# A shared ring of weight slots that is no longer cut short near the end of a layer

## The chip, the cores and the metric

The kernel runs on one core of a Trainium2 chip. The metric is device time in microseconds (us) of one execution, as the median of several timed runs. The profile is of one further execution; "span" is the time from its first to its last instruction.

## The reference, cut to what matters

A two-layer trunk. In each layer a mixer (gated linear attention, a Fourier mix and windowed attention, merged through gates) is followed by a hierarchical mixture of 16 experts. Layer 0 works on 512 rows (256 of x, 256 of the context), layer 1 on 256.

```python
def hierarchical_moe(h, w_router_group, w_router_expert, w1, w3, w2):
    ...
    out = jnp.zeros(h.shape, h.dtype)
    for e in range(MOE_EXPERTS):          # 16
        hid = jax.nn.silu(h @ w1[e]) * (h @ w3[e])
        out = out + (hid @ w2[e]) * gates[:, e:e + 1]
    return out

def trunk_layer(x, xc, ...):
    ...
    x = x + gate1[:, None, :] * y
    h2 = modulate(rms_norm(x, g_ffn), shift2, scale2)
    x = x + gate2[:, None, :] * hierarchical_moe(h2...)
```

Each token has two experts, so most products of the loop are zero. `w1[e]` and `w3[e]` are 1024 x 512, `w2[e]` is 512 x 1024, all in float32.

## The kernel before

The experts run as 16 places, in an order by their number of tokens. A place is big (B, up to 128 tokens, products of split high and low halves) or small (s, up to 64 tokens, plain float32 products of two weight halves side by side): `PLACES`, line 30, "BBBBsBBsBBsBBsss" in layer 0 and "BBBsssBssssBssss" in layer 1. The last three places are small in both layers.

**The weights** of one place come as six pieces of 1 MB, two each of w1, w3 and w2, 96 pieces a layer. `pieces_of` (line 1266) yields them in the order of use: of place q the second pieces of w1 and w3, then the first pieces of place q+1, then the two of w2 of place q. `wload` (239, its DMA has line 245) issues each load on SP's queue, which is worked off in order; a load whose slot is still being read holds all that stand behind it. Numbered #1 to #96, the last are: #85 and #86 w2 of place 13, #87 and #88 second w1 and w3 of place 14, #89 and #90 first w1 and w3 of place 15, #91 and #92 w2 of place 14, #93 and #94 second w1 and w3 of place 15, #95 and #96 w2 of place 15.

**The ring.** `ring` (1256) gives each piece the next slot in turn, 8 KB a partition. Layer 0 has 12 slots, in this order from #1: six of `ra`, two of `raw`, two of `rb0`, two of `rb1`. Layer 1 has 13: the free half of `x` first, six of `ra`, two of `raw`, one each of `rc`, `rb0`, `rb1`, `rc`. The four slots of `rb0`, `rb1` and `rc` are the spare ones (`self.spare`, 1383), marked True. `ring` counts pieces; once the count is over `CUT` = 84, spare slots that come to the head are dropped, so that layer 0 goes on with 8 slots and layer 1 with 9. The four spare slots then serve, in order, the outputs of places 14 and 15 (`last_y`, 1666) and the first two row blocks that are read back (`rows`, 1755).

**A small place** on TensorE: `pair` (line 1643) with w1 and w3, a first half for the next place in `begin` (1646) and a second half in the loop (1676). Then ACT copies and takes tanh (1693, 1655), DVE multiplies twice (1656, 1657), TensorE transposes (1662), DVE copies (1697), and TensorE takes w2 (`pair` again, written to tile `c`). Outputs of places 0 to 13 are scattered to the DRAM tensor `yb` by GpSimd's queue (1561). Those of 14 and 15 stay in memory as two halves each (ACT 1731, DVE 1732) and are put onto their rows by products with a one-hot tile `oh` (1774). The rows of `yb` are read back on SP's queue (1758), their two halves added on GpSimd (1759), added on TensorE by a product with the identity (1777), and the sum goes through gate and addition into x (1795, 1797). A branch (1783) to a general path for overfull experts stands before that; it isn't taken in the profile.

**Order and memory.** The kernel is written in a tile framework that orders each engine's instructions ahead of the run, by place in the source and by its own reckoning of when an instruction's inputs are there, and adds the semaphores. Pools are stacked on a left and a right side; a new tile waits until the tiles that lay on its bytes have been read. `ra` is on the left, after `moed`; `rb0` and `rb1` are on the right. Layer 1 opens `hhi`, `hlo`, `early`, then `ong` and `ssum` on the left where `moed` and `ra` of layer 0 lay. Its first steps are the norm of x (416, 407, 408, 525), transposes (537), scale and shift (546), the split into `hhi` (GpSimd, 550) and `hlo` (DVE, 551), and the first products (228).

Of the kernel before, what the change touches and what calls it, by code (L numbers as in the profile page):

```python
# [8 lines left out]
F32 = mybir.dt.float32  # L9
F32R = mybir.dt.float32r  # L10
# [9 lines left out]
P = 128  # L20
# [10 lines left out]
RING = (6, 7)  # L31
ONCE = (0, 2)
AHEADG = 2
CUT = 84
EXTRA = 2
EA = 8
EB = 1
# [77 lines left out]
def ts(i, n):  # L115
    return slice(i * n, (i + 1) * n)
# [12 lines left out]
class Net:  # L129
# [461 lines left out]
    def mixer(self, l, filler):  # L591
# [20 lines left out]
        if l:  # L612

            h = [hp.tile([P, 2, KD, SEQ], F32R, name=n) for n in ("hhi", "hlo")]
# [16 lines left out]
        s1 = ExitStack()  # L631
        yc = self.swa(s1)
        self.dump(f"y2{l}", yc[0].bitcast(F32))
        self.rings, self.ahead, self.slots, self.piece, self.gen = [], [], [], 0, self.pieces_of(l)
        if l:

            self.rings = [(Slot(self.x[:, 2:4].rearrange("p t d -> p (t d)")), False)]
            self.ahead = [next(self.gen) for _ in self.rings]
            n = EXTRA
            self.raws += [self.raw] + [self.pool(sh, "raw2", bufs=n)] * n  # L640
# [590 lines left out]
    def moe_pre(self, l, T, ww):  # L1231

        nt, ns = T // P, T // SEQ
        self.sh = ExitStack()
        self.dp = self.pool(self.sd, "moed")
        self.pos = self.dp.tile([P, 5, NE], F32, name="pos")
        self.nc.sync.dma_start(self.pos, self.io["k_pos"][:, l])
        self.h2b = self.dr.tile([T, D], F32, name=f"h2b{l}")
        n = RING[l] - len(self.slots + self.rings)
        new = [(t, False) for t in self.slots] + [(self.pool(self.sd, "ra", bufs=n), False)] * n  # L1240
        self.rings = new + [(self.raw, False)] * 2 + self.rings
        self.once = [self.pool(self.sd, "rc", bufs=ONCE[l])] * ONCE[l] if ONCE[l] else []
        if self.once:
            ww.append(self.wload(self.io["w_out"][l][:, ts(3, 256)], KD, 256, self.once[0].tile([P, 2048], F32, name="wraw")))
        self.sx = ExitStack()
        self.xp = xp = self.pool(self.sx, "moex")
        self.h2 = xp.tile([P, nt, D], F32, name="h2")
        self.oh0 = xp.tile([P, nt, CAP[l]], F32, name="oh0")
        self.hp = hp = self.pool(self.sh, "moeh", side="right")
        self.xtr = [hp.tile([P, 2, 2, P], F32, name=f"xtr{i}") for i in range(3)]  # L1250
        self.g2 = self.mod_bcast(hp, l, 2, ns, "gm2")
        self.s2 = self.mod_bcast(hp, l, 1, ns, "sh2")
        self.ssq = hp.tile([P, ns, 2, 4], F32, name="ssq")
        self.pieces = chain(self.ahead + [next(self.gen) for _ in new], self.gen)

    def ring(self):

        self.piece += 1
        if self.piece > CUT:

            while self.rings[0][1]:
                self.rings.pop(0)
        self.rings.append(self.rings.pop(0))
        return self.rings[-1][0].tile([P, 2048], F32, name="wraw")

    def pieces_of(self, l):

# [108 lines left out]
    def moe_ahead(self, l):  # L1376


        n = 2 - l
        y1 = self.pool(self.sd, "rb1", bufs=n, side="right")  # L1380
        y0 = self.pool(self.sd, "rb0", bufs=n, side="right")

        self.spare = self.once[1:] + [y0] * n + [y1] * n + self.once[:1]
        self.rings[2:2] = [(p, True) for p in self.spare]
        gen = self.pieces

        first = [next(gen) for _ in range(len(self.rings) - ROWS[l].count("w"))]
        last = self.wd
        for o in ROWS[l]:
            if o == "w":  # L1390
                with self.tc.issue_after(last.ins):
                    first.append(next(gen))
                last = self.wd
            else:
                self.behind(self.hw[int(o)], last)
                last = self.hw[int(o)]
        self.pieces = chain(first, gen)
        self.got, self.cut, self.parts = {}, {}, 6
        self.cut["w1", 0, 0] = list(self.halves("w1", 0, 0))

    def moe(self, l):
# [263 lines left out]

        def last_y(e):

            ye = self.spare.pop(0).tile([P, 2048], F32, name="wraw").bitcast(F32R).rearrange("p (h d) -> p h d", h=2)
            yes.append(ye)
            return ye  # L1670
        p1 = begin(0, xx)
        for e in range(NE):
# [34 lines left out]
            if e == NE - 2:  # L1707
# [9 lines left out]
                rq = self.pool(sr, "rows2", bufs=2, side="right") if nt > 2 else None  # L1717
            if not big[e]:
                p2 = self.c2()
                for c in range(2):  # L1720
                    w = self.piece_at("w2", e, c)
                    for k in range(2):
                        pair(p2, hs, [w[:, k:k + 1, ts(o, 512)] for o in range(2)], (2 * c + k, 4), 1)
                if e < NE - 2:
                    ye = yp.tile([P, 512], F32, name="ye")
                    nc.scalar.activation(ye, p2, AF.Copy, scale=gsl[:, e:e + 1])  # L1726
                    put = (ye, e)
                    continue

                ye = last_y(e)[:, :, :512]  # L1730
                nc.scalar.activation(ye[:, 0], p2, AF.Copy, scale=gsl[:, e:e + 1])
                V.scalar_tensor_tensor(ye[:, 1], p2, gsl[:, e:e + 1], ye[:, 0].bitcast(F32), op0=OP.mult, op1=OP.subtract)
                continue
# [7 lines left out]
            if e < NE - 2:  # L1741
                ye = yp.tile([P, D], F32, name="ye")
                for o in range(2):
                    nc.scalar.activation(ye[:, ts(o, 512)], p2[o], AF.Copy, scale=gsl[:, e:e + 1])
                put = (ye, e)
                continue
            ye = last_y(e)
            for o in range(2):
                q = ts(o, 512)
# [4 lines left out]

        def rows(t):

            yr = (self.spare.pop(0) if t < 2 else rq).tile([P, 2048], F32, name="wraw").rearrange("p (r d) -> p r d", r=2)
            nc.sync.dma_start(yr, yb.rearrange("(r q) d -> q r d", r=2)[ts(t, P)])
            i = nc.gpsimd.tensor_add(yr[:, 0], yr[:, 0], yr[:, 1])
            self.adds += [i] if t >= 2 else []  # L1760
            return yr
        self.adds, self.lates = [], []
        yrs = [rows(t) for t in range(nt)]

        def put_rows(t, pt, js):
# [16 lines left out]
        n = nc.values_load(cnti[0:1, 0:1], min_val=0, max_val=T)  # L1782
# [3 lines left out]
        for t in range(nt):  # L1786
            self.pri.append(tc.cur_priority)
            yr = yrs[t]
# [125 lines left out]
```

## Time and profile before

| | |
|---|---|
| median of three timed runs | 1590.89 us (1585.81 to 1591.39) |
| profiled execution | 1584.03 us, its span 1582.0 us |
| PE, matmuls | 1452.4 us busy, 92% |
| DVE, ACT, POOL | 942.1, 752.1, 232.5 us busy |
| DMA | 363.14 MB, mean 230 GB/s |
| weight pieces of the experts | 192 loads of 1024 KB on SP's queue |
| experts of layer 0, experts of layer 1 | end near 940 us, near 1563 us |

The page gives the busy time of each engine, then the span in 40 slices of 39.55 us. A busy TensorE is not yet one at its peak, and the DMA digit is a mean over 16 DMA engines. SP is not counted as busy: its waits are read from its own view of the waits. A line such as L1643 or L245 belongs to a helper that many steps share, so a stretch of time has to go with it.

### The profile page before, as it was taken

The numbers are of one execution on the slowest core, as the hardware profiler recorded it, in microseconds if no ns is written. First come the engines' busy times: TensorE is split into PE (matmuls) and PEld (weight loads), VectorE is DVE, ScalarE is ACT, GpSimd is POOL, SyncE is SP. The second block draws the span as 40 slices with busy tenths as digits, with TensorE's granted clock in tenths as the row PEclk, the third lists the DMA queues.
The fourth block names the chain that finished last, engine by engine and source line by source line (L and its number), as shares of the span: only waits on it lengthen the run. The fifth ranks groups of instructions, "written<-read, shape, count | busy, mean of one in ns | idle before, by whom it ended". The sixth has DMA issues, their size and how long they took to land. (4 is left out here: it accounts for less than half of the span.)

```text
span 1582.0 us, 22237 instructions
## 1 busy us (share of the span) xinstructions
PE 1452.4 (92%) x8141; PEld 1020.5 (65%) x8141; DVE 942.1 (60%) x1753; ACT 752.1 (48%) x1292; POOL 232.5 (15%) x244
## 2 busy tenths in 40 slices
PE   6999899999999997899998979999899979998885
PEld 4666666577777796676675427687689967453421
DVE  4479667532376786797775417467965679251412
ACT  4668556422223233586665306668654548241411
POOL 2025100000021103111110014023001121121001
PEclk9999999999999997999999988999999989999998
DMA  9762242443556578699999763322336689999992
GB/s 321 214 208 92 91 150 81 145 138 110 198 174 214 187 234 311 214 357 388 391 369 369 289 256 116 122 90 81 105 100 200 214 309 337 370 384 393 395 373 89
DMA packets 218505, 363.14 MB, mean 230 GB/s; under 512 B 25676, under 2 KB 100630, under 8 KB 218388
## 3 DMA queue, kind: packets, MB, share of 16 engines
q1 hardware_dynamic: 211520, 349.77, 63.6%
q0 software_dynamic: 6432, 11.76, 2.1%
q8 instruction: 67, 1.10, 0.3%
q14 instruction: 50, 0.41, 0.1%
q10 hardware_dynamic: 436, 0.10, 0.0%
HBM read 350.56 MB, written 21.82 MB: 235 GB/s over the span
## 5 line engine op out<-in xcount | busy, mean ns | idle before, releaser
L266 DVE TENSOR_TENSOR wlo<-wraw,whi 128x1024 fp32r<-128x1024 f32 (+1 forms) x324 | 377.2, 1177 | 186.3 <-ACT whi L265 121.5
L265 ACT ACTIVATE whi<-wraw 128x1024 fp32r<-128x1024 f32 (+1 forms) x324 | 321.7, 1009 | 239.4 <-PE pa L229 114.6
L228 PE MATMUL pa<-hhi,whi 128*128 128x512 f32 (+1 forms) x704 | 240.6, 356 | 1.8 <-ACT qT L788 1.0
L229 PE MATMUL pa<-hlo,whi 128*128 128x512 f32 (+1 forms) x704 | 237.6, 352 | 0.0
L228 PEld LDWEIGHTS pa<-hhi,whi 128*128 128x128 f32 x704 | 133.3, 189 | 36.5 <-issue 16.0
L1643 PE MATMUL pa<-wraw,xh 128*64 128x512 f32 x520 | 151.4, 636 | 0.0
L231 PE MATMUL pa<-hhi,wlo 128*128 128x512 f32 (+1 forms) x704 | 151.0, 348 | 0.0
L229 PEld LDWEIGHTS pa<-hlo,whi 128*128 128x128 f32 x704 | 133.4, 190 | 22.6 <-issue 9.6
L231 PEld LDWEIGHTS pa<-hhi,wlo 128*128 128x128 f32 x704 | 113.4, 190 | 20.2 <-issue 6.2
L763 POOL TENSOR_TENSOR m<-m,gu 128x512 f32<-128x512 f32 (+1 forms) x32 | 39.3, 1228 | 402.7 <-DVE gu L761 402.7
L1656 DVE SCALAR_TENSOR_TENSOR th<-th,pa 64x512 f32<-64x512 f32 (+1 forms) x32 | 21.7, 679 | 124.2 <-ACT th L1655 124.2
L1643 PEld LDWEIGHTS pa<-wraw,xh 128*64 128x64 f32 x520 | 42.8, 144 | 76.5 <-issue 74.5
L235 PE MATMUL pa<-whi,xh 128*128 128x512 f32 x208 | 85.0, 408 | 7.4 <-ACT whi L265 6.9
L236 PE MATMUL pa<-wlo,xh 128*128 128x512 f32 x208 | 85.8, 413 | 2.9 <-DVE wlo L266 2.8
L237 PE MATMUL pa<-whi,xl 128*128 128x512 f32 x208 | 83.4, 401 | 0.0
L1555 POOL DMA_INDIRECT xg<-h2b,tki x30 | 35.7, 1190 | 264.5 <-PE c L1618 94.6
L1643 PE MATMUL c<-wraw,hh 128*64 128x512 f32 x256 | 72.6, 634 | 1.0 <-DVE hh L1697 1.0
L236 PE MATMUL pa<-y,whi 128*128 128x512 f32 (+1 forms) x192 | 66.3, 345 | 0.9 <-DVE y L272 0.9
L235 PE MATMUL pa<-y,whi 128*128 128x512 f32 (+1 forms) x192 | 65.5, 341 | 0.7 <-DVE mx L1143 0.7
L237 PE MATMUL pa<-y,wlo 128*128 128x512 f32 (+1 forms) x192 | 65.1, 339 | 0.0
L349 DVE SCALAR_TENSOR_TENSOR adaw<-adaw,cT 128x512 f32<-128x512 f32 x56 | 49.1, 877 | 15.8 <-DMA adaw<-in_w_ada_dram 15.2
L1561 POOL DMA_INDIRECT yb<-ye,yki x28 | 28.5, 1018 | 198.5 <-ACT ye L1726 109.1
(458 smaller groups left out, 2817.5 us busy)
## 6 DMA issues: line engine op xcount, KB each, us to landing
wraw<-in_w_dram SPq DMA_DIRECT2D x184, 1024.0 KB
wraw<-in_w_in_dram SPq DMA_DIRECT2D x44, 1024.0 KB
adaw<-in_w_ada_dram SPq DMA_DIRECT2D x80, 512.0 KB
adaw<-in_w_ada_dram SPq DMA_DIRECT2D x8, 1024.0 KB
wraw<-in_w_out_dram SPq DMA_DIRECT2D x8, 1024.0 KB
x<-in_w_dram SPq DMA_DIRECT2D x8, 1024.0 KB
yb<-zero SPq DMA_DIRECT2D x12, 512.0 KB
wraw<-yb SPq DMA_DIRECT2D x6, 1024.0 KB
```

Source lines behind the costliest of these rows:

```text
L228: mm(out, lh, rh, start=(i == 0), stop=False)
L229: mm(out, lh, rl, start=False, stop=False)
L231: self.mm = mm(out, ll, rh, start=False, stop=(i == len(ops) - 1))
L235: mm(out, lh, rh, start=start, stop=False)
L236: mm(out, lh, rl, start=False, stop=False)
L237: self.mm = mm(out, ll, rh, start=False, stop=stop)
L265: self.sp = nc.scalar.activation(hv[:, :, q], v[:, :, q], AF.Copy)
L266: self.sl = self.lo.tensor_sub(lv[:, :, q], v[:, :, q], hv[:, :, q].bitcast(F32))
L349: nc.vector.scalar_tensor_tensor(v[:, j], v[:, j], ck, acc, op0=OP.mult, op1=OP.add)
L763: nc.gpsimd.tensor_add(self.m[:, j, :], self.m[:, j, :], u[:, :TY])
L1555: return nc.gpsimd.indirect_dma_start(out=xgs[e % len(xgs)][:n], out_offset=None, in_=h2b, in_offset=bass.IndirectOffsetOnAxis(ap=tki[:n, ...
L1643: nc.tensor.matmul(ps[ts(i, SM)], xs[:, k0[0] + k, :], w[:, k, :], start=(k0[0] + k == 0), stop=(k0[0] + k == k0[1] - 1))
```

## The change

The mark on ring entries, the count and the cut go. All slots stay in the ring to the end of the layer, and what took spare slots by name now takes the ring's next slot at its place in the source: the output of place 14 between #92 and #93, that of place 15 and row blocks 0 and 1 after #96. In layer 0 the slots are then: output of place 14 that of #81 (as before), #93 to #95 those of #82 to #84, #96 that of #85, output of place 15 that of #86, row blocks those of #87 and #88. In layer 1: #88 to #91 those of #75 to #78, #92 that of #79, output of place 14 that of #80, #93 to #96 those of #81 to #84, output of place 15 that of #85, row blocks those of #86 and #87 (`raw`).

```diff
-CUT = 84
@@ mixer
-        self.rings, self.ahead, self.slots, self.piece, self.gen = [], [], [], 0, self.pieces_of(l)
+        self.rings, self.ahead, self.slots, self.gen = [], [], [], self.pieces_of(l)
         if l:
-            self.rings = [(Slot(self.x[:, 2:4].rearrange("p t d -> p (t d)")), False)]
+            self.rings = [Slot(self.x[:, 2:4].rearrange("p t d -> p (t d)"))]
@@ moe_pre
-        new = [(t, False) for t in self.slots] + [(self.pool(self.sd, "ra", bufs=n), False)] * n
-        self.rings = new + [(self.raw, False)] * 2 + self.rings
+        new = self.slots + [self.pool(self.sd, "ra", bufs=n)] * n
+        self.rings = new + [self.raw] * 2 + self.rings
@@ ring
-        self.piece += 1
-        if self.piece > CUT:
-
-            while self.rings[0][1]:
-                self.rings.pop(0)
         self.rings.append(self.rings.pop(0))
-        return self.rings[-1][0].tile([P, 2048], F32, name="wraw")
+        return self.rings[-1].tile([P, 2048], F32, name="wraw")
@@ moe_ahead
-        self.spare = self.once[1:] + [y0] * n + [y1] * n + self.once[:1]
-        self.rings[2:2] = [(p, True) for p in self.spare]
+        self.rings[2:2] = self.once[1:] + [y0] * n + [y1] * n + self.once[:1]
@@ last_y
-            ye = self.spare.pop(0).tile([P, 2048], F32, name="wraw").bitcast(F32R).rearrange("p (h d) -> p h d", h=2)
+            ye = self.ring().bitcast(F32R).rearrange("p (h d) -> p h d", h=2)
@@ rows
-            yr = (self.spare.pop(0) if t < 2 else rq).tile([P, 2048], F32, name="wraw").rearrange("p (r d) -> p r d", r=2)
+            yr = (self.ring() if t < 2 else rq.tile([P, 2048], F32, name="wraw")).rearrange("p (r d) -> p r d", r=2)
```

## Rows read from the trace of the kernel before

**Rows 1.** The page, part 2: DMA busy tenths in 40 slices.
```profile
DMA  9762242443556578699999763322336689999992
```

**Rows 2.** Waits of SP's queue, 885 to 935: who, for whom, total us, times, longest.
```profile
SPq L245 <- PE c L1643: 16.2, 2, 15.1
...
SPq L1758 <- DMA yb<-ye,yki: 3.8, 1, 3.8
```

**Rows 3.** The same view, 1495 to 1550.
```profile
SPq L245 <- PE c L1643: 13.3, 4, 10.5
```

**Rows 4.** Windows: length; busy us (instructions) by engine; granted clock, DMA share, GB/s.
```profile
902.90:908.00 5.10, 5.10 (x26) 1.66 (x24) 0.00 (x0) 0.00 (x0) 0.00 (x0) 0.94 0.07 12
908.00:920.70 12.70, 9.84 (x36) 3.08 (x32) 1.78 (x3) 1.87 (x3) 0.99 (x1) 0.73 1.01 373
...
1513.00:1517.70 4.70, 4.70 (x25) 1.57 (x23) 0.00 (x0) 0.69 (x1) 0.99 (x1) 1.00 0.74 268
1517.70:1544.50 26.80, 21.07 (x88) 6.87 (x86) 3.58 (x6) 3.54 (x6) 0.98 (x1) 0.87 1.03 393
```

**Rows 5.** Timeline of SP: start us, us, instruction, out<-in, count; three narrow windows.
```profile
906.33 0.37 SPq L245 DMA_DIRECT2D wraw<-in_w_dram  x1
...
910.64 1.22 SPq L245 DMA_DIRECT2D wraw<-in_w_dram  x2
...
915.71 1.99 SPq L1758 DMA_DIRECT2D wraw<-yb  x4
```

**Rows 6.** Timeline of PE, layer 0; in brackets idle time before and what ended it.
```profile
892.39 4.50 PE L1643 MATMUL pa<-wraw,xh 128*64 128x512 f32 x18
...
907.43 4.03 PE L1643 MATMUL pa<-wraw,xh 128*64 128x512 f32 x17
914.32 0.66 PE L1662 MATMUL c<-ident,th 64*128 64x64 f32 x4 [2.86 <-DVE th L1657]
...
925.57 0.50 PE L1774 MATMUL pa<-wraw,oh 64*128 64x512 f32 x1 [0.78 <-ACT wraw L1731]
...
926.36 0.73 PE L1774 MATMUL c<-wraw,oh 64*128 64x512 f32 x3
927.02 3.65 PE L1643 MATMUL pa<-wraw,xh 128*64 128x512 f32 x14
...
934.49 5.21 PE L1643 MATMUL c<-wraw,hh 128*64 128x512 f32 x16 [0.52 <-DVE hh L1697]
```

**Rows 7.** Timeline of SP in layer 1: the last weight piece.
```profile
1533.14 0.37 SPq L245 DMA_DIRECT2D wraw<-in_w_dram  x1
```

**Rows 8.** Timeline of PE, layer 1.
```profile
1541.95 4.02 PE L1643 MATMUL c<-wraw,hh 128*64 128x512 f32 x15
...
1549.06 3.65 PE L1643 MATMUL pa<-wraw,xh 128*64 128x512 f32 x14
...
1556.74 6.40 PE L1643 MATMUL c<-wraw,hh 128*64 128x512 f32 x16 [0.52 <-DVE hh L1697]
```

**Rows 9.** Waits of PE, 893 to 942: total us, times, longest.
```profile
PE c L1662 <- DVE th L1657: 4.8, 2, 2.9
```

**Rows 10.** Waits of PE, 1500 to 1565.
```profile
PE c L1662 <- DVE th L1657: 7.7, 3, 2.9
```

**Rows 11.** Timelines of DVE, PE and POOL where layer 0 ends.
```profile
939.78 0.07 DVE L779 MEMSET ssum<- 128x8 f32 x1 [5.35 <-PE c L1643]
...
949.65 2.36 DVE L1797 TENSOR_TENSOR x<-x,wraw 128x1024 f32<-128x1024 f32 x2 [2.89 <-DVEq L1783]
...
951.22 3.66 PE L1774 MATMUL c<-wraw,oh 64*128 64x512 f32 x9 [3.34 <-PEq L1783]
...
959.31 0.85 PE L537 MATMUL pf<-ident,xr 128*128 128x128 f32 x3
...
959.46 0.61 POOL L550 TENSOR_SCALAR hhi<-hf 128x512 fp32r<-128x512 f32 x1
```

**Rows 12.** Windows again: the granted clock after a hole of PE.
```profile
914.00:920.00 6.00, 5.68 (x16) 1.98 (x18) 0.59 (x2) 0.00 (x0) 0.00 (x0) 0.50 1.03 415
```

## The prediction, made before the changed kernel was run

> **What bounds the kernel now.** I read four things in this order. First the page's DMA row: the DMA engines are full (digit 9) for most of the two expert stages, around slices 17 to 22 and 33 to 38 [rows 1]. So a change that lets weights come sooner could pay, if TensorE waits for weights where the change acts. It acts only where CUT acts: from the 85th weight piece of a layer on (I write #85; each layer has 96 pieces of 1 MB, six for each of 16 places).
>
> Second, the DMA queue's own waits. In layer 0 SP stands 15.1 us in one wait before a weight load, released by a matmul of the helper's line L1643 [rows 2]; in layer 1 10.5 us [rows 3]. The ring's arithmetic says which. Layer 0 has 12 slots: six of `ra`, two of `raw`, four spare. #93 comes to the first spare slot, all four are popped, and #93 must wait for the slot of #85, the first w2 piece of place 13. Layer 1 has 13 slots (`x` is one), and there #88 is the first, waiting for #79. So the reduction to 8 and 9 slots is real. While SP waits, DMA runs dry: 0.07 busy from 902.9 to 908, against 1.01 after it [rows 4]; in layer 1 it only thins to 0.74, against 1.03 after [rows 4].
>
> Third, whether anybody waits for those late pieces. In layer 0 the last four are issued from 906.33 to 911.5 [rows 5], and the queue moves 12.7 us x 373 GB/s = 4.7 MB from 908 to 920.7 [rows 4]: #93 to #96 (4.2 MB) are in by about 921. TensorE gets to them later: it is on #87 and #88 from 907.43, transposes place 14 at 914.32, puts most of #93 and #94 from 927.02 and #95 and #96 from 934.49 [rows 6]. In layer 1 the last piece is issued at 1533.14 [rows 7], and 26.8 us x 393 GB/s = 10.5 MB go by from 1517.7 to 1544.5 [rows 4], more than #88 to #96 (9.4 MB) and the 0.5 MB of `gb`; TensorE starts #94 at about 1549 and #95 at 1556.74 [rows 8].
>
> Fourth, what TensorE does wait for there: the gate arithmetic of each small place. 4.8 us in two waits before the transposes L1662 in layer 0 [rows 9], 7.7 us in three in layer 1 [rows 10], all ended by DVE's product L1657, none by a DMA. So the last three places are held by TensorE and by the chain matmul, ACT, DVE, transpose, with weights some 5 to 13 us ahead.
>
> **The change part by part.** *The ring.* No instruction is added or removed on any engine; the same 192 loads go through the same queue. In layer 0 place 14's output keeps the slot of #81, #93 to #95 take those of #82 to #84, #96 that of #85, place 15's output that of #86, the rows those of #87 and #88. #82 is read to the end of the run of 18 that starts at 892.39 [rows 6], about 896.9, so #93 can be issued some 9 us sooner, right behind #92. With the 5.1 us hole gone [rows 4] the last weights land near 916 instead of 921. In layer 1 #88 needs #75 instead of #79 and is issued sooner too, but DMA is still emptying its backlog there: its hole is 0.26 x 4.7 = 1.2 us, and the later pieces come that much sooner. Gain at TensorE: zero in both layers, as it starts these pieces after they have landed already.
>
> *The outputs.* Place 15's output, and in layer 1 place 14's, are written into slots whose pieces are read long before (in layer 0 #86, done by 907.5; the output is written after 939.7). No wait; zero.
>
> *The rows.* In layer 0 they need #87 and #88 read out; the run of 17 from 907.43 ends at 911.46 [rows 6]. They are issued at 915.71 [rows 5], after a 3.8 us wait for the scatter of place 13 [rows 2], so the scatter is last, before and after; I leave the time at 915.71. With the queue empty by then they land up to 5 us sooner. They are used only in L1777, after #96, so zero. Behind them on SP stands only the branch at L1783 and the next layer's first two loads; what can be gained there is cover, not time. In layer 1 the same, with `raw` slots.
>
> *What is moved past.* Ring slots on the left side of memory now hold live tiles to the end of the layer. The next layer's `hhi`, `hlo`, the `early` tiles, `ong` and `ssum` open on just those bytes (the pools' sizes are unchanged: `moed`, then 48 KB of `ra`, against 16 + 16 + 8 + 4 KB). The trace shows such sharing: DVE's memset of `ssum` at 939.78 stands until the last w2 matmul, 5.35 us [rows 11]. After the change `ssum` lies under row block 1, so its 0.07 us go behind the addition to x at 949.65 to 952.01 [rows 11], on the path: +0.07 us. `hhi` lies under place 15's output, last read by the nine L1774 matmuls that end at 954.88, and is first written at 959.46 [rows 11]: 4.6 us of cover, cost zero; without the cover, see the third rival. `hlo` lies under row block 0, free with the same addition. Ends of this unknown: -0.1 us (the memset leaves its old place ahead of the eviction of place 15 and falls into an idle time) and +8.1 us (third rival); I take +0.1, as the memset has a row and the rival needs the cover gone.
>
> *Sum.* 0 + 0 + 0.1 on the profiled 1584.03 us. The profile is 6.9 us under the median of 1590.89 and near the fastest timed run, 1585.81; the four executions scatter by more than the change. On the median: 1591.0.
>
> **The rivals.**
> *A, the matmuls change their order (faster).* The program's order of instructions is planned ahead, and the plan reckons with when a piece comes. Between #92 and #94 stand six L1774 matmuls, from 925.57 on, after a hole of 0.78 us [rows 6], which come later in the source: a sign that the plan saw #94 late, though it had landed. If it now sees it in time, #93 and #94 follow #92 at once. Their end moves from 927.02 + 3.65 = 930.67 to 925.57 - 0.78 + 3.65 = 928.44, 2.2 us; in layer 1 from 1549.06 + 3.65 = 1552.71 to 1545.97 + 3.65 = 1549.6, 3.1 us [rows 8]. The L1774 then fill the gate's wait. That is 1590.9 - 5.3 = 1585.6. If the shorter hole also keeps the clock up, the last w2 runs (5.21 and 6.40 us [rows 6, 8]) shrink to the 4.3 us that layer 1 needs for 16 at full clock (4.02 for 15 [rows 8]): another 3.0, 1582.6. The clock does follow holes: granted 0.50, the lower of its two levels (1.2 of 2.4 GHz), from 914 to 920 [rows 12], after the 2.86 us hole before 914.32 [rows 6]. Against A: a plan that is short of DMA throughput, not of slots, sees #94 no sooner, because loads follow each other without a hole however deep the ring is.
>
> *B, the ring is what makes the holes (faster).* The waits of rows 9 and 10 repeat at each small place; closing them all gives 4.8 + 7.7 = 12.5 us, 1578.4. Against it stands the releaser in both rows, DVE's arithmetic, and the landed weights. The Trainium skill's page Perfetto Trace Analysis, section Optimization Strategy, reads a gap that repeats on the busiest engine as possibly too little memory for the next tile, which is this rival. By that rule 1578.4, by the rows no change; the trace does not agree with it here.
>
> *C, memory held longer stops the next layer (slower).* `hhi` waits for place 15's output. If the nine L1774 are put behind the transposes of the next layer, which run to 959.31 + 0.85 = 960.16 [rows 11], they end at 960.2 + 3.66 = 963.8 and `hhi` starts 4.4 us late: 1595.3; at half clock another 3.7, 1599.0. It decides from the point where those nine end after 959.46. Now they end at 954.88, so 4.6 us must be lost first.
>
> *That it doesn't do what it says:* were #93 held by something else in SP's order, the hole in DMA would stay and the time too; same number as the forecast.
>
> **How the numbers follow.** No change 0.62, A 0.18, B 0.06, C 0.14. Likeliest: 1591.0, with the scatter of the timed runs about 1586 to 1594 by itself. The range 1582 to 1596 takes in A and the first price of C and leaves out B, a little of A and C's upper part, under 0.2 in all. A measurement of this kernel can tell about 0.5% from no change, that is under 1582.9 or over 1598.9. Faster: B, a third of A, and 0.02 of unknown, 0.14. Slower: a third of C and 0.03 of unknown, 0.08. Same: 0.78.
>
> **What would show it.** DMA busy share near 1 between 903 and 908 and the issue of #93 near 897 show the ring doing what it says. TensorE's waits before L1662 unchanged and still ended by DVE show that nobody waited for weights. A is shown by L1643 x16 in one run before any L1774; C by the start of `hhi` against the end of L1774. The forecast is wrong if TensorE's start of #95 moves by over 3 us against the start of #87 in either layer, or the stretch from the last w2 matmul to the next layer's first L228 matmul changes by over 3 us.

## The result: 8 us slower, and the profile after

| | before | after |
|---|---|---|
| median | 1588.89 us (20 runs) | 1596.02 us (20 runs) |
| ratio, with its 95% interval | 1 | 1.0054 (1.0040 to 1.0069) |
| again, beside the experiments | 1586.80 us (29 runs) | 1596.33 us (6 runs), 1.0054 (1.0033 to 1.0076) |
| span of the profiled execution | 1582.0 us | 1592.5 us |
| PE, DVE, ACT, POOL busy | 1452.4, 942.1, 752.1, 232.5 us | 1456.5, 945.7, 751.9, 230.6 us |
| DMA | 363.14 MB | 363.15 MB |

The forecast was 1591.0 us, no change. The interval says 6 to 11 us more. The number of instructions is the same on every engine, so the time is in their order, and in the clock that TensorE has meanwhile (it is busy 4.1 us longer). The lines of the changed kernel are those of before less 7 (less 1 ahead of the edit in `ring`): L1774 is now L1767, L1777 is L1770, L1783 is L1776, L245 is L244.

The page's DMA row of after answers to [rows 1]: the same but for single digits.
```profile
DMA  9762342443556678699999663323235689999983
```
Two rows of after answer to [rows 2, 4]: the wait of SP in 891 to 946, and the window in which the hole lies.
```profile
SPq L1751 <- DMA yb<-ye,yki: 20.4, 1, 20.4
...
902.90:908.00 5.10, 5.10 (x26) 1.69 (x24) 0.00 (x0) 0.00 (x0) 0.00 (x0) 0.99 0.00 0
```
The hole isn't closed: DMA is now idle in all of it. SP stands 20.4 us, not before a weight load but before row blocks, which wait for the scatter of place 13. The timeline of SP in after (it answers to [rows 5]) shows the new order.
```profile
911.87 0.89 SPq L1751 DMA_DIRECT2D wraw<-yb  x2
913.02 4.30 SPq L244 DMA_DIRECT2D wraw<-in_w_dram  x4
920.27 7.63 SPq L244 DMA_DIRECT2D wraw<-in_w_in_dram  x2
936.86 0.89 SPq L1751 DMA_DIRECT2D wraw<-yb  x2
```
Before, SP's order was #93 to #96, row blocks 0 to 3, the branch, then the next layer's loads of w_in. Now it is row blocks 2 and 3, #93 to #96, two loads of w_in, the branch, and only then row blocks 0 and 1: issued at 936.86 where they were issued at 915.71. Why the plan puts row blocks 2 and 3 ahead of #93 wasn't tested. The timelines of TensorE and VectorE in after (they answer to [rows 6, 11]) show what that does:
```profile
926.00 3.65 PE L1636 MATMUL pa<-wraw,xh 128*64 128x512 f32 x14 [0.74 <-DMA wraw<-in_w_dram]
...
933.46 5.35 PE L1636 MATMUL c<-wraw,hh 128*64 128x512 f32 x16 [0.52 <-DVE hh L1690]
...
946.28 0.80 PE L1767 MATMUL pa<-wraw,oh 64*128 64x512 f32 x2 [5.95 <-PEq L1776]
946.85 4.18 PE L1767 MATMUL c<-wraw,oh 64*128 64x512 f32 x10
950.96 3.59 PE L1770 MATMUL pa<-wraw,ident 128*128 128x512 f32 x4
954.38 1.88 PE L1770 MATMUL c<-wraw,ident 128*128 128x512 f32 x4
...
939.58 0.75 DVE L1725 SCALAR_TENSOR_TENSOR wraw<-c,gsl,wraw 128x512 fp32r<-128x512 f32 x1 [6.17 <-ACT wraw L1724]
953.07 0.69 DVE L1788 TENSOR_TENSOR wraw<-pa,gb 128x512 f32<-128x512 f32 x1 [12.74 <-PE pa L1770]
...
957.77 1.23 DVE L1790 TENSOR_TENSOR x<-x,wraw 128x1024 f32<-128x1024 f32 x1
```
and those of before, with rows that weren't shown:
```profile
941.70 1.98 PE L1777 MATMUL pa<-wraw,ident 128*128 128x512 f32 x4
...
944.05 1.98 PE L1777 MATMUL c<-wraw,ident 128*128 128x512 f32 x4
...
940.47 0.75 DVE L1732 SCALAR_TENSOR_TENSOR wraw<-c,gsl,wraw 128x512 fp32r<-128x512 f32 x1 [0.62 <-ACT wraw L1731]
942.87 0.69 DVE L1795 TENSOR_TENSOR wraw<-pa,gb 128x512 f32<-128x512 f32 x1 [1.65 <-PE pa L1777]
...
946.07 0.69 DVE L1795 TENSOR_TENSOR wraw<-c,gb 128x512 f32<-128x512 f32 x1 [0.17 <-PE c L1777]
```
In both, place 15's output is evicted at about the same time (DVE, 940.47 and 939.58). Before, TensorE went on at once: products with row blocks 0 and 1 (L1777), the four gated products on DVE done at 946.76, then the branch, then the two additions to x, done at 952.01 [rows 11]. After, both engines meet the branch first. TensorE stands 5.95 us at it, then does the last two put matmuls (L1767, the one-hot products) of row block 0 and ten more, eight of them for row blocks 2 and 3, and takes row block 0 at 950.96; the second addition to x ends at 959.00.

To compare executions I cut each one at events that every kernel has: the start of GpSimd's last scatter in layer 0, the end of DVE's eviction of place 15, the end of the second addition to x, and the start of the transposes of vT in layer 1 (TensorE, L881; the first of them some 72 us on). The first and the last of these rows, before and after:
```profile
909.01 0.99 POOL L1561 DMA_INDIRECT yb<-ye,yki  x1 [14.47 <-ACT ye L1726]
...
1023.61 0.66 PE L881 MATMUL c<-ident,vT 128*128 128x128 f32 x4 [2.04 <-ACT vT L878]
```
```profile
909.21 0.98 POOL L1554 DMA_INDIRECT yb<-ye,yki  x1 [14.47 <-ACT ye L1719]
...
1032.28 0.72 PE L880 MATMUL c<-ident,vT 128*128 128x128 f32 x4 [2.05 <-ACT vT L877]
```
That is 114.60 against 123.07 us: 8.5 us are lost here, as much as the timed runs lose. Where a kernel was profiled twice, the sum of the three stretches came out the same within 0.3 us (e6 apart, whose last w2 run had another clock), though a single execution takes some 4 us more or less in all. Between kernels that are the same in layer 0 the sum still differs by up to 1.1 (before 114.6, e9 114.5, e2 113.5). So the table below is the measure, in us, and the timed runs stand beside it. "1" is the last scatter to the eviction of place 15, "2" the eviction to the second addition, "3" the addition to vT; "end" is the start of the last scatter of layer 1 to the end of DVE's last instruction. Each ratio is against runs of the kernel before in the same group of runs.

| kernel | 1 | 2 | 3 | sum | end | timed ratio (95%) |
|---|---|---|---|---|---|---|
| before | 32.2 | 10.8 | 71.6 | 114.6 | 46.1 | 1 |
| after | 31.1, 32.0 | 18.7, 17.6 | 73.3, 73.2 | 123.1, 122.8 | 46.9, 48.1 | 1.0054 (1.0040 to 1.0069) |
| e1, change in layer 0 alone | 31.3 | 18.7 | 73.1 | 123.2 | 47.6 | 1.0050 (1.0034 to 1.0067) |
| e2, change in layer 1 alone | 30.6 | 11.0 | 72.0 | 113.5 | 45.7 | 1.0007 (0.9992 to 1.0022) |
| e4, before, row loads behind the branch | 30.4 | 17.6 | 72.9 | 120.9 | 46.4 | 1.0048 (1.0029 to 1.0066) |
| d1, before, branch first | 32.0, 32.2 | 13.5, 13.3 | 72.0, 71.9 | 117.5, 117.4 | 47.9, 46.5 | 1.0001, 1.0003 (0.9985 to 1.0021) |
| e7, after, row loads in time | 32.3, 32.3 | 14.2, 14.4 | 73.4, 73.5 | 119.9, 120.1 | 47.9, 46.9 | 1.0043, 1.0041 (1.0025 to 1.0056) |
| e8, after, branch behind products | 32.2, 31.2 | 10.6, 11.9 | 73.4, 73.2 | 116.2, 116.3 | 41.3, 42.0 | 0.9995, 0.9994 (0.9979 to 1.0010) |
| e9, before, the same hold | 32.1 | 10.8 | 71.6 | 114.5 | 44.6 | 0.9979 (0.9961 to 0.9998) |
| n1, before, no branch | 32.1 | 7.0 | 71.4 | 110.4 | 42.4 | 0.9939 (0.9919 to 0.9958) |
| n2, after, no branch | 32.3 | 8.5 | 73.1 | 114.0 | 41.7 | 0.9956 (0.9938 to 0.9975) |
| e6, before, put matmuls held | 28.6, 25.2 | 10.8, 10.8 | 71.6, 71.6 | 111.0, 107.6 | 43.2, 42.7 | 0.9950, 0.9957 (0.9936 to 0.9978) |
| b3, after, put matmuls held | 31.2 | 18.7 | 73.1 | 123.0 | 41.4 | 1.0044 (1.0025 to 1.0063) |
| b1, after, both held | 31.3 | 11.7 | 73.2 | 116.1 | 41.3 | 0.9989 (0.9976 to 1.0002) |
| b2, before, both held | 28.6 | 11.1 | 71.6 | 111.3 | 41.1 | 0.9933 (0.9910 to 0.9956) |

Where two values stand, the kernel was profiled twice; the interval is then that of the second group of runs, for after that of the first.

### The profile page after: what moved, and what is told of

It reads as the page before. It is cut to its first block, busy times and chain, and to the rows that moved or that the text cites. A ratio compares the mean times of both kernels' runs of the same rounds, so it can differ in the third digit from the quotient of the medians.

```text
span 1592.5 us, 22232 instructions
## 1 busy us (share of the span) xinstructions
PE 1456.5 (91%) x8141; PEld 1022.5 (64%) x8141; DVE 945.7 (59%) x1753; ACT 751.9 (47%) x1292; POOL 230.6 (14%) x244
## 2 busy tenths in 40 slices
DMA packets 218507, 363.15 MB, mean 228 GB/s; under 512 B 25677, under 2 KB 100631, under 8 KB 218389
## 5 line engine op out<-in xcount | busy, mean ns | idle before, releaser
L265 DVE TENSOR_TENSOR wlo<-wraw,whi 128x1024 fp32r<-128x1024 f32 (+1 forms) x324 | 380.5, 1188 | 185.7 <-ACT whi L264 123.3
L228 PE MATMUL pa<-hlo,whi 128*128 128x512 f32 (+1 forms) x704 | 238.6, 353 | 0.7 <-DVE hlo L550 0.7
L228 PEld LDWEIGHTS pa<-hlo,whi 128*128 128x128 f32 x704 | 134.0, 190 | 23.8 <-issue 9.4
L1636 PE MATMUL pa<-wraw,xh 128*64 128x512 f32 x528 | 148.1, 626 | 0.7 <-DMA wraw<-in_w_dram 0.7
```

The source lines that it names most:

```text
L228: mm(out, lh, rl, start=False, stop=False)
L265: self.sl = self.lo.tensor_sub(lv[:, :, q], v[:, :, q], hv[:, :, q].bitcast(F32))
L1636: nc.tensor.matmul(ps[ts(i, SM)], xs[:, k0[0] + k, :], w[:, k, :], start=(k0[0] + k == 0), stop=(k0[0] + k == k0[1] - 1))
```

## The experiments

**Which layer, and which part.** Four kernels. My first theory, T: row blocks 0 and 1 come late on the chip, because a pool hands its slots out in the order in which its tiles are first written in the source, and in layer 0 these blocks now take `ra` slots behind place 15's output. Its rivals: M, the memory that the ring holds on the left (rival C of the prediction), and L, the tail of layer 1.

e1 and e2 have, in place of `CUT = 84`, `CUT = (999, 84)` and `CUT = (84, 999)` by layer, and take the outputs' and the row blocks' slots from `ring` in that layer alone.

> The kernel before, with the change made in layer 0 alone; layer 1 keeps the cut ring and its kept-aside slots. Theory T (late rows): the loss sits in layer 0, where row blocks 0 and 1 are now read behind the branch at the layer's end; so nearly all of the slowdown is here: 7 to 9 us over before, the first L228-type matmul of layer 1 some 6 to 7 us later than before. Rival M (memory): slots on the left held to the end of the layer stop the next layer's first tiles; it expects the same 7 to 9 us here, and differs from T only in the last two kernels of this group. Rival L (layer 1's tail, where the rows' load now stands ahead of the last four weights and waits 15 us): 0 to 1 us.

> The kernel before, with the change made in layer 1 alone. T and M: 0 to 1 us over before (layer 0 is as before; in layer 1 the last four weights are issued some 17 us later than before but still in time, and no layer follows). Rival L: 7 to 9 us over before.

e1 measured 1.0050 with the whole 8.6 us in the three stretches, e2 1.0007. The loss is at the end of layer 0.

e4 is the kernel before with one thing moved:
```diff
-        yrs = [rows(t) for t in range(nt)]
+        yrs = {t: rows(t) for t in range(2 * (l == 0), nt)}
...
+        yrs.update({t: rows(t) for t in range(nt) if t not in yrs})
         self.pri = []
```


> The kernel before with its cut ring and its kept-aside slots, but in layer 0 the loads and additions of row blocks 0 and 1 are written behind the branch at the layer's end, so that they are issued there. T: this alone costs what the change costs in layer 0, 7 to 9 us over before. M: within 1 us of before, as no slot on the left is held longer than before.

1.0048, 6.3 us in the stretches: with the cut ring and no slot held longer. So the ring isn't needed for the loss. But T isn't right as it stands either. In e4 both additions on GpSimd are done at 937.74, before TensorE has even reached the branch:
```profile
932.84 2.35 POOL L1759 TENSOR_TENSOR wraw<-wraw 128x1024 f32<-128x1024 f32 x1 [22.40 <-DMA wraw<-yb]
935.39 2.35 POOL L1759 TENSOR_TENSOR wraw<-wraw 128x1024 f32<-128x1024 f32 x1 [0.20 <-issue]
...
943.50 0.50 PE L1774 MATMUL pa<-wraw,oh 64*128 64x512 f32 x2 [3.66 <-PEq L1783]
943.80 2.56 PE L1774 MATMUL c<-wraw,oh 64*128 64x512 f32 x7
946.65 1.44 PE L1774 MATMUL c<-wraw,oh 64*128 64x512 f32 x3 [0.28 <-issue]
948.02 3.41 PE L1777 MATMUL pa<-wraw,ident 128*128 128x512 f32 x4
```
The row blocks are there, and TensorE still crosses the branch and does the same ten put matmuls first. Late is what the planner takes them for; it is the order, fixed ahead of the run, that costs.

e7 is the changed kernel with the two loads written ahead of place 15's output:
```diff
+            if e == NE - 1:
+                self.early = [read(self.ring(), t) for t in range(2)]
             ye = self.ring().bitcast(F32R)...
...
```


> The changed kernel, with only the two loads of row blocks 0 and 1 written ahead of place 15's output, so that they take their slots in the same pool before it and are issued ahead of the branch. The ring, the late issue of the last four weights and the slots held on the left stay as in the changed kernel. T: the loss of layer 0 is gone, 0 to 2 us over before. M: the same 7 to 9 us over before as the changed kernel.

Now SP issues them at 922.56, ahead of its branch. That agrees with the slot order of T (same pool, earlier first use, earlier load), but the loads also stand earlier in the source here, so the slot order isn't shown by itself. The time was 1.0043, against what T expected, and it looked like M. The trace says otherwise: stretch 2 falls from 18.7 to 14.2 us (the ten matmuls no longer stand ahead), and the branch is still first.

**The place of the branch.** Theory B took T's place: the engines cross the branch before the work on row blocks 0 and 1 and not after it. e8 undoes that in the changed kernel, with `issue_after`, which puts an instruction behind another on its engine:
```diff
...
+        for t in range(2):
+            put_rows(t, pts[t], (1,))
+            done = products(t, pts[t])
+        with tc.issue_after(self.put.ins), tc.issue_after(done[1].ins):
+            n = nc.values_load(cnti[0:1, 0:1], min_val=0, max_val=T)
-        n = nc.values_load(cnti[0:1, 0:1], min_val=0, max_val=T)
         with tc.If(n > 0):
...
```


> The changed kernel, with one thing undone in its order: every engine's branch at the end of the layer is held behind the two gated products of row blocks 0 and 1, as it stands in the kernel before. The ring, the slots held on the left, the late issue of the last four weights and the two w_in loads that now run ahead of the row blocks all stay. Theory B (branch order): the change costs time because TensorE and VectorE now cross the branch before the work on row blocks 0 and 1 and not after it; with that undone the loss is gone but for some 2 us that the earlier split of the w_in weights costs: 0 to 3 us over before. Theory M (memory held on the left): 5 to 9 us over before, as in the changed kernel.

Level with before, 0.9995. The DVE timeline of e8 has the order of before again, and the second addition ends 10.6 us after the eviction:
```profile
942.26 0.75 DVE L1725 SCALAR_TENSOR_TENSOR wraw<-c,gsl,wraw 128x512 fp32r<-128x512 f32 x1 [6.03 <-ACT wraw L1724]
944.90 0.69 DVE L1777 TENSOR_TENSOR wraw<-pa,gb 128x512 f32<-128x512 f32 x1 [1.89 <-PE pa L1770]
...
951.24 2.36 DVE L1793 TENSOR_TENSOR x<-x,wraw 128x1024 f32<-128x1024 f32 x2 [2.93 <-DVEq L1783]
```
M is out: the ring, the slots on the left and the late weights are all still there. e8 doesn't move the branch alone, though: SP now issues row blocks 0 and 1 ahead of its own branch as well (929.49, where in after it was 936.86). e4 and d1 take the two apart.

n1 and n2 leave the branch and the path behind it out of both kernels, so their times are those of less work.

> The kernel before without the branch at the end of a layer: the path for tokens over the capacity, which this input does not take, is left out in both layers. B: the crossing costs what VectorE stands there between its last product and the first addition to x, 2.9 us in layer 0; so 2 to 6 us under before (two layers).

> The changed kernel without the branch at the end of a layer (the same path left out). B: most of the distance between the two kernels goes with the branch; against the kernel before without its branch it is 1 to 5 us slower (eight matmuls of the other row blocks still stand ahead of the product's matmuls, and the split of the w_in weights is still early), not 7 to 9. M: 7 to 9 us slower than the kernel before without its branch.

n2 is 3.5 us longer than n1 in the three stretches, and its median is 2.0 us over that of n1: with the branch 5.0 of the 8.5 us between the kernels are gone. n1 gained more than expected, 10 us: 4.2 of it in the stretches and 3.7 at the end of layer 1.

d1 makes the reverse test in the kernel before: the branch at high priority, right behind the eviction.
```diff
...
+        with tc.high_priority(300):
+            with tc.issue_after(self.evict.ins):
+                n = nc.values_load(cnti[0:1, 0:1], min_val=0, max_val=T)
+            with tc.If(n > 0):
+                self.moe_general(l, T, h2b, gun, gund, gb)
```


> The kernel before, its cut ring, its slots and its loads in their old order, with one edit: the branch at the end of the layer is planned right behind VectorE's eviction of place 15, so that every engine crosses it before the work on row blocks 0 and 1, as in the changed kernel. Theory B: the place of the branch costs this by itself: 3 to 7 us over before. If late row blocks are needed for the loss as well: within 1.5 us of before.

By the trace +2.9 us, by the clock 1.0001 (0.9978 to 1.0023): under what B expected (3 to 7 us). The place of the branch alone isn't the loss.

> The changed kernel again, on the same chip as the next three, as their measure: 6 to 10 us over before.

> The changed kernel with the branch held behind the products, again. If the place of the branch and what follows from it (late row blocks, the other blocks' matmuls ahead of theirs) is the whole loss but for the early split of w_in: 0 to 2 us over before, 5 to 9 under the changed kernel. If the first result was luck: 3 to 5 us over before.

> The earlier kernel with the branch first and the row blocks in time, again. If the place of the branch costs what the trace shows between the eviction of place 15 and the second addition to x (13.5 against 10.8 us): 2 to 4 us over before. If it is free as long as the row blocks are in time, as its first times say: within 1.5 us.

> The changed kernel with the row blocks read ahead of the branch (in time) and the branch still first, again. By the trace the place of the branch and the early split of w_in make 5 us over before (4 to 6); by its first times 8 (7 to 9), and then 3 us of it are still without a cause.

Side by side all four came out as before: 1.0054, 0.9994, 1.0003, 1.0041. d1's interval ends at 1.0021, 3.3 us, which takes in its traced 2.8; e7's begins at 4 us, which takes in its traced 5.5.

That e8 is level with before while its stretches are 1.6 us longer had to be explained. In layer 1 the kernel before crosses the branch ahead of the products already, as its TensorE rows show (VectorE has just left the branch, and L1777 comes behind it):
```profile
1564.94 0.50 PE L1774 MATMUL pa<-wraw,oh 64*128 64x512 f32 x2 [0.28 <-DVEq L1783]
1565.37 0.70 PE L1777 MATMUL pa<-wraw,ident 128*128 128x512 f32 x1
1567.79 1.55 PE L1777 MATMUL pa<-wraw,ident 128*128 128x512 f32 x3 [1.72 <-issue]
```
e8 changes that as well. e9 puts the same hold into the kernel before, where layer 0 has it already.

> The kernel before with its branch held behind the gated products of row blocks 0 and 1 in both layers. In layer 0 it stands there already, so only layer 1 changes. If the place of the branch costs in layer 1 as well: 1 to 5 us under before, and from the last scatter to the end 41 to 43 us where the kernel before has 46. If not: within 1.5 us of before.

0.9979 (0.9961 to 0.9998), 3 us under before, in its trace 1.5 us at the end of layer 1, less than expected. That e8 gains in layer 1 about what it still loses in layer 0 fits the times, but the traces don't show the place of the branch as the reason. Of the 4.8 us by which "end" is shorter in e8 than in before, 2.75 are the last w2 run, which stands ahead of the branch: it had the full clock in both executions of e8, and took 6.40 us in before [rows 8] and 5.35 in e9. The row of e8:
```profile
1559.27 3.65 PE L1636 MATMUL c<-wraw,hh 128*64 128x512 f32 x16 [0.51 <-DVE hh L1690]
```
Of the 1.5 us of e9, 1.05 are that run too. From its end to DVE's last instruction before takes 14.5 us, e9 14.5 and e8 14.6 and 14.4; against after (17.5 and 17.3) e8 is shorter there.

**The first rival's price.** e6 is the kernel before with the first put matmuls of place 14 (L1774, six between #92 and #94) held behind the last matmul on #94.
```diff
...
+                        if not j and t < 2:
+                            self.behind(i, lastup)
...
```


> The kernel before, with only the first put matmuls of place 14's output (six stand between #92 and #94) held behind the last matmul on #94, so that they fill TensorE's wait for place 15's gate arithmetic. By the first rival of the forecast: 2 to 5 us under before. By its main reading (TensorE and the gate chain in turn): within 2 us of before, if the six matmuls then delay the transposes of place 15 instead.

> The earlier kernel with the put matmuls of place 14's output held behind the last matmul on #94, again, as the measure for the next two: 5 to 10 us under before.

0.9950 and 0.9957, 7 to 8 us faster. Place 15 gets its weights and its gate arithmetic runs while TensorE does the six; in the second execution the last w2 run also had the full clock, 3.65 us for 16 where before it took 5.21 [rows 6].

> The changed kernel with the same hold of the put matmuls. B: the hold saves its 5 to 10 us here too and the place of the branch still costs its 7 to 9, so within 3 us of before, and 6 to 10 us over the hold on the kernel before.

> The changed kernel with the hold of the put matmuls and with the branch held behind the gated products of row blocks 0 and 1. B, with a ring that brings nothing by itself: the same as the hold on the kernel before, within 3 us of it (5 to 10 us under before). If the deeper ring brings weights that TensorE would otherwise wait for, once the put matmuls no longer stand in between: over 3 us under the hold on the kernel before.

> The kernel before with the hold of the put matmuls and the hold of the branch together. If the two add: 8 to 12 us under before. If the hold of the put matmuls has already taken what layer 1 gives: the same as that hold alone, 5 to 9 us under before.

On the changed kernel the same hold brings next to nothing, against what B expected: b3 is 7 us over before, not within 3, and b1, with both holds, is at 0.9989, 5 to 9 us over the hold on the kernel before (by the ratios and by the medians), not within 3. In b3 "end" is 5.5 us shorter than in after, of which 1.6 are again the last w2 run at full clock; the timed ratios lie only some 1.6 us apart. b2, both holds on the kernel before, is at 0.9933. One thing that takes the gain away on the changed kernel is seen in the TensorE rows of b1 and of e6: #93 and #94, issued late, are now waited for.
```profile
928.29 3.65 PE L1636 MATMUL pa<-wraw,xh 128*64 128x512 f32 x14 [1.26 <-DMA wraw<-in_w_dram]
```
```profile
921.98 4.02 PE L1643 MATMUL pa<-wraw,xh 128*64 128x512 f32 x15
```
In layer 1 TensorE waits 1.87 us in b1 and 1.83 in b3 at the same place, by the profile for SP's queue. In the stretches b1 is 4.9 us over b2, of which 2.7 are stretch 1; the two ratios lie 9 us apart, and the other 4 us aren't seen there and stay open. b2, 1578.84 us, is the fastest complete kernel of this study, 10.6 us under before, with the short ring: there the two holds add, as expected.

## Why the prediction failed

**The step that failed is the order of SP's queue, and with it the term "The rows", which the sum has at zero.** That term measured 7.9 us in stretch 2 (6.9 in the second execution). "The same 192 loads go through the same queue" is true of the loads, not of their order. "The scatter is last, before and after; I leave the time at 915.71" took the order in the source as the order of issue. Row blocks 0 and 1 were issued at 936.86, row blocks 2 and 3 went ahead of #93, and #93 was issued at 913.02, 6.7 us later than before, not 9 sooner. I had written the planner down in the section on the kernel, and used it only for rival A. Where a planner orders the instructions, a slot's new owner is an input to the plan: the row blocks shared a pool with nothing that was still to be written before, and share one with place 15's output now (that this is what moved them is argued; e7 agrees with it).

**The second missing term is the branch.** It stands in the rows I read: 2.89 us of DVE and 3.34 us of PE, both ended by L1783 [rows 11]. I named it only as something that stands behind the rows on SP and costed the edit at nothing, without asking on which side of the branch the work on row blocks 0 and 1 would be. In after it is on the far side. The 7.9 us of stretch 2 then divide as follows, each from one kernel against another: the branch ahead of the products, 2.6 to 2.7 (d1); the ten put matmuls ahead of row block 0, 4.1 (e4 over d1; in the rows of e4 they take the 4.2 us from 943.80 to 948.02); and the rest, 1.1 (after over e4; nothing in the second execution of after), where TensorE's crossing is 5.95 us (4.86) against 3.66 in e4, so that part of the longer crossing is won back behind it. Without any branch the late order costs 1.6 us in stretch 2 (n2 against n1, 8.55 against 6.95; the row blocks are issued at 927.25 there), so most of the loss is the two together.

**Stretch 3** adds 1.7 us. In after, e1, e4, e7, e8, n2, b1 and b3 VectorE splits two pieces of w_in (L265; L266 in e1 and e4) ahead of `hlo`, in before, d1, e2, e6, e9, n1 and b2 one piece behind half of `hlo` (L266). After, then before:
```profile
964.19 4.92 DVE L265 TENSOR_TENSOR wlo<-wraw,whi 128x1024 fp32r<-128x1024 f32 x2
969.04 1.69 DVE L550 TENSOR_TENSOR hlo<-hf,hhi 128x512 fp32r<-128x512 f32 x2
```
```profile
961.31 0.69 DVE L551 TENSOR_TENSOR hlo<-hf,hhi 128x512 fp32r<-128x512 f32 x1 [0.51 <-POOL hhi L550]
961.92 1.22 DVE L266 TENSOR_TENSOR wlo<-wraw,whi 128x1024 fp32r<-128x1024 f32 x1
```
The kernels with the early split are 1.3 to 1.9 us longer there, the others within 0.5 of before. Which edit moves the split isn't settled: e4 has it without the ring, e7 and e8 with it. Place 15 gives 1.1 us back in after (stretch 1), though not in its second execution.

**Point by point.** The reading of the profile held: nobody waited for late weights. The hole in DMA grew, #93 came 6.7 us later, and TensorE waited 0.74 us for a weight. That "zero" was right, for a ring that did the opposite of what I said. The outputs at zero: nothing in the traces speaks against it. The memset of `ssum` did go behind the addition to x, at 959.07, at no visible price. Rival C did not happen: the last L1767 run, which reads place 15's output, ends at 959.32, and `hhi` is first written at 966.46, 7.1 us of cover where I saw 4.6; it starts 7.5 us after the second addition to x in both kernels. Rival B did not happen either: the waits of [rows 9, 10] stand at the same 4.8 and 7.7 us, ended by DVE. The fourth rival, "#93 held by something else in SP's order", is what SP did; "the time too" was its error. Rival A was right as a mechanism and in its price (5.3 us, 8.3 with the clock; measured 7 to 8), but the ring doesn't bring it about, and its late weights take it away (TensorE's waits for them in b1 and b3). Its second price had a wrong term: 16 matmuls of a w2 run at full clock take 3.65 us (e6, second execution), not 4.3. My own test said where to look: the stretch from the last w2 matmul to the first L228 of layer 1 was to change by under 3 us. It went from 963.79 - 939.70 = 24.1 to 970.44 - 938.81 = 31.6, 7.5 us more.

**Chances.** Slower by over 0.5% had 0.08. Its only named mechanism was memory held on the left. A rival "the plan puts the row blocks behind the branch" could have been priced from [rows 11] alone: 3.34 us of crossing and the nine L1774 of 3.66 us ahead of the products, 7 us, 1598.

## What to carry to other kernels

Where a framework plans the order, a change of which pool a tile comes from is a change of the order of every queue: price each instruction that waits for that tile at the next control-flow boundary behind it, not at its old place. Look for engine time that ends at a branch: the work that it cuts off from its inputs is worth more than the branch itself, and an explicit order (branch behind the products, put matmuls behind the weights) was worth 10 us here, where four more slots a layer were worth none.

## What the runs showed of the hardware

At the end of layer 0 the branch that jumps over the general path costs TensorE 3.2 to 5.95 us and VectorE, where its wait is seen, 2.9 to 3.2 us ([rows 11], e8, b2). The windows show the crossing and what comes behind it, in the columns of [rows 4]: after (crossing, behind it), before (crossing, behind it), d1 (crossing, behind it).
```profile
940.30:946.20 5.90, 0.03 (x2) 0.00 (x0) 0.03 (x1) 0.00 (x0) 3.60 (x2) 0.81 0.56 225
946.30:954.40 8.10, 8.10 (x17) 4.58 (x18) 0.69 (x1) 0.00 (x0) 0.99 (x1) 0.51 0.02 4
```
```profile
947.90:951.20 3.30, 0.00 (x0) 0.01 (x1) 1.55 (x2) 0.29 (x1) 0.00 (x0) 1.00 0.03 7
951.30:954.80 3.50, 3.50 (x9) 2.28 (x9) 2.05 (x5) 1.91 (x4) 1.54 (x3) 0.50 0.03 5
```
```profile
941.90:945.70 3.80, 0.00 (x0) 0.00 (x0) 0.00 (x0) 0.00 (x0) 0.00 (x0) 0.91 0.04 11
945.80:951.00 5.20, 5.20 (x9) 1.79 (x9) 1.37 (x2) 0.00 (x0) 0.00 (x0) 0.50 0.03 6
```
TensorE crosses in 3.2 to 4.1 us where DMA is all but idle (share 0.02 to 0.05: before, e2, e4, e6, e8, e9, d1, b1, b2) and in 4.9 to 5.95 us where it is busy (0.46 to 0.60: after, e1, e7, b3; the lowest pair is the second execution of after). The Trainium skill, on the page Runtime: NRT & Kernel Launch, section Instruction fetch mechanics, says that a taken branch to a target outside the prefetched window waits for a DMA fetch of that page. The two groups agree with it; no run varied the DMA load alone, so it isn't shown.

Not every crossing is long. At the end of layer 1 TensorE's branch instruction takes 0.43 us in before and in after, where in layer 0 it takes 3.49 and 5.85 us. The row of before for both layers, with least, median and largest ns:
```profile
L1783 PEldq COMPARE_BRANCH  x2: 426/1958/3491, 947.4 to 1564.3; - x2
```
There TensorE then has a gap of 1.72 us a few matmuls on, for which the profile names no other engine, and VectorE waits 0.4 us (e8 and e9, behind the products). ScalarE is past the branch in 0.4 us in layer 0 too (before, 940.3 to 940.7). What makes a crossing long stays open.

Behind the three crossings in the windows the granted clock is 0.50 or 0.51, the lower of TensorE's two levels (1.2 of 2.4 GHz), after it has stood still for 3.3 to 5.9 us. Four matmuls on a row block take 3.59 us (after) where they take 1.98 us at full clock (before). So the work that was put behind the branch took longer there than ahead of it. Leaving the branch out of both layers was worth 10 us.
